# Scoring the short ranges of a gated linear recurrence with 32x32 products in four column groups

## The chip, the cores and the metric

The kernel runs on one NeuronCore of a Trainium2 chip. The metric is the device time of one execution in microseconds (us). Each core has a matrix engine (TensorE, PE in the profile, with its weight loads shown as PEld), a vector engine (DVE), a scalar engine (ACT), a general engine (POOL) and a queue engine (SP). Matrix products write to PSUM, which is eight banks of 512 float32 columns on 128 partitions. Three executions of the kernel before took 1450.94, 1452.36 and 1452.39 us.

## The reference

One residual block of a hybrid encoder: 1024 tokens, 1024 channels, float32. The normalised input is projected to two branches. The first is a stick-breaking attention with 8 heads. The second, around which the change lies, is a gated linear recurrence (HGRN2) with 4 heads of 128 channels:

```python
bcum = jnp.cumsum(gi, axis=2)
diff = bcum[:, :, :, None, :] - bcum[:, :, None, :, :]
decay = jnp.exp(jnp.where(causal[:, :, None], diff, -jnp.inf))
scores = jnp.einsum('bhtd,bhsd,bhtsd->bhts', qi, ki, decay)
o = jnp.einsum('bhts,bhse->bhte', scores, vi) \
    + jnp.einsum('bhtd,bhde->bhte', qi * jnp.exp(bcum), state)
```

Here `gi` is the logarithm of the forget gate, `ki` one minus the gate, and a state is carried from chunk to chunk. Both branches are gated, added and projected, and a squared-ReLU MLP (1024 to 4096 to 1024) and a norm follow.

## The kernel before, in words

Everything is transposed so that channels lie on partitions and tokens in columns; the recurrence works in 8 chunks of 128 tokens. Most products split each float32 operand into a high and a low part of type float32r and add three products (`three`, L526). The recurrence's score products are taken in plain float32.

Within a chunk the score of a pair (s, t) carries the product of the gates between them. The kernel builds it level by level (`hg_levels`, L969). At level l blocks of 2H tokens, H = 2^l, are halved. A key in the left half has been multiplied by the gates up to the end of its half, a query in the right half by the gates from its start, so a plain product of left keys with right queries gives the scores between the halves. After it, `k`, `q` and the running gate products in `dec` are multiplied on DVE for the next level (L1055 to L1057), in two halves of 512 tokens. Seven levels (H = 1 to 64) and the diagonal make a chunk complete. The score tile `sc` has 8 chunks of 128 columns.

The parts of a head before are these. The diagonal and the levels H = 1 and 2 (l = 0 and 1; the sums of a level are formed and laid in the step after it) multiply pairs element by element on DVE (`pairs_of`, L987), split the result in high and low, and sum over channels by a product with a 128x128 tile of ones (`sums_of`, L995). The diagonal's sums are multiplied by the identity into `sc`, and those of l = 0 and 1 are laid by a predicated copy (`lay`, L1010). Levels l = 2, 3, 4 (H = 4, 8, 16) take the whole 128x128 product of each chunk (`scores_of`, L976) and keep the part under a mask (L1070). Levels l = 5 and 6 (H = 32, 64) take only the blocks between halves, as 32x32 and 64x64 products that all write PSUM partitions from 0 upward (L1044), and ACT copies them into `sc` (L1076). `make_masks` (L936) builds the masks once.

Two lanes set PE's order. Blocks opened with `open_block("main")` follow each other as written; blocks of `fill` (the projections, the merge gate's products and others, kept in a stream of jobs) are let in between by a manual dependency on an earlier main block. After each `yield` of the levels or of the tail, the loop at L2168 advances the stream by `FILL[h]` steps (3.75 for the first head); a step of a projection is 2 of 8 channel tiles, 6 passes on PE. The tail of head h - 1 (`hg_tail`, L1079) alternates with the levels of head h: it turns keys, builds the chunk states, multiplies `sc` with the values, normalises (POOL takes the root) and gates. Tiles of 1024 columns come from a pool of 40 slots, tiles of up to 512 columns from a pool of 10; a new tile waits for the release of the one whose place it takes. `turn_lo[0]` is the last remainder that the attention issues on DVE.

Of the kernel before, what the change touches and what calls it, by code (L numbers as in the profile page):

```python
# [9 lines left out]
F32 = mybir.dt.float32  # L10
F32R = mybir.dt.float32r
I32 = mybir.dt.int32
U8 = mybir.dt.uint8
AF = mybir.ActivationFunctionType
ALU = mybir.AluOpType
# [4 lines left out]
P = 128  # L20
T = 1024
D = 1024
NT = T // P
# [16 lines left out]
def kernel(  # L40
# [19 lines left out]
    nc = tc.nc  # L60
# [7 lines left out]
    cpool = ctx.enter_context(tc.tile_pool(name="consts", bufs=1))  # L68
# [6 lines left out]
    def slot(name, dt=F32):  # L75
        return spool.tile([P, 1024], dt, tag="s", name=name)

    def slot_n(name, n, dt=F32):

        if n <= 512:  # L80
            return hpool.tile([P, 512], dt, tag="h", name=name)
        return slot(name, dt)

    def bank(name):
        return psum.tile([P, 512], F32, tag="p", name=name)
# [12 lines left out]
    def after(ins, earlier):  # L98
        if earlier is not None and earlier.ins is not ins.ins:
            tc.add_manual_dep(ins.ins, earlier.ins.name, NOSYNC, reason="issue order")  # L100
        return ins
# [18 lines left out]
    def matmul(*a, **k):  # L120
        return pe(nc.tensor.matmul(*a, **k))  # L121
# [30 lines left out]
    def hi_lo(h, l, src):  # L152
        hi_copy(h, src)
        return lo_sub(l, src, h)

    def mul(out, a, b):
        return nc.vector.tensor_tensor(out=out, in0=a, in1=b, op=ALU.mult)  # L157

    def halves():
        return ((i, slice(i * 512, (i + 1) * 512)) for i in range(2))  # L160

    ident = cpool.tile([P, P], F32, tag="ident", name="ident")
# [764 lines left out]

    hg_jobs(0)

    ones = cpool.tile([P, P], F32R, tag="ones", name="ones")  # L930
    nc.gpsimd.memset(ones.bitcast(F32), 1.0)


    masks = []

    def make_masks():  # L936
        mscr = slot_n("mscr", 4 * P, I32)
        m_x, m_s, m_gt, m_odd = (mscr[:, i * P : (i + 1) * P] for i in range(4))
        nc.gpsimd.iota(m_x, pattern=[[1, P]], base=0, channel_multiplier=0)
        nc.gpsimd.iota(m_s, pattern=[[0, P]], base=0, channel_multiplier=1)  # L940
        nc.vector.tensor_tensor(out=m_gt, in0=m_x, in1=m_s, op=ALU.is_gt)
        nc.vector.tensor_scalar(out=m_odd, in0=m_s, scalar1=1, scalar2=None, op0=ALU.bitwise_and)
        nc.vector.tensor_tensor(out=m_x, in0=m_x, in1=m_s, op=ALU.bitwise_xor)

        def add_mask(l, m_if):
            nc.vector.tensor_scalar(
                out=m_s, in0=m_x, scalar1=l, scalar2=None, op0=ALU.logical_shift_right
            )
            m = bits[:, len(masks) * P : (len(masks) + 1) * P]
            nc.vector.scalar_tensor_tensor(  # L950
                out=m, in0=m_s, scalar=1.0, in1=m_if, op0=ALU.is_equal, op1=ALU.mult
            )
            masks.append(m)

        for l in (0, *range(2, 5)):
            add_mask(l, m_gt)

        mul(m_odd, m_odd, m_gt)
        add_mask(1, m_odd)
        nc.vector.tensor_tensor(out=m_odd, in0=m_gt, in1=m_odd, op=ALU.subtract)  # L960
        add_mask(1, m_odd)

    def chunks(t):
        return t.rearrange("p (c t) -> p c t", t=P)

    def over_chunks(t):
        return t.unsqueeze(1).to_broadcast([P, 4, P])

    def hg_levels(h):  # L969

        dec, k, q = (hg[h, n] for n in ("pp", "k", "q"))
        sc = hg[h, "sc"] = slot(f"sc{h}")

        def scores_of(name):  # L976
            open_block("main")
            banks = []
            for half in range(2):
                S = bank(f"{name}_{half}")  # L980
                for c in range(4):
                    cs = slice((4 * half + c) * P, (4 * half + c + 1) * P)
                    matmul(S[:, c * P : (c + 1) * P], k[:, cs], q[:, cs], start=True, stop=True)
                banks.append(S)
            return banks

        def pairs_of(name, n, *products):  # L987

            t, h_, l_ = (slot_n(f"{name}_{x}", n, d) for x, d in zip("xhl", (F32, F32R, F32R)))
            for (a, b, w), (i, cs) in zip(products, halves()):  # L990
                mul(t[:, cs].rearrange("p (n c) -> p n c", c=w) if w else t[:, 0:n], a, b)
            after(hi_lo(h_, l_, t), turn_lo[0] if "sd0" in name else None)
            return name, n, h_, l_

        def sums_of(pairs):  # L995

            name, n, h_, l_ = pairs
            open_block("main")
            banks = []
            for c0 in range(0, n, 512):  # L1000
                S = bank(f"{name}_{c0}")
                matmul(S, ones, h_[:, c0 : c0 + 512], start=True, stop=False)
                matmul(S, ones, l_[:, c0 : c0 + 512], start=False, stop=True)
                banks.append(S)
            return banks

        def blocks_of(t, H):
            return t.rearrange("p (n two h) -> p n two h", two=2, h=H)

        def lay(mask, S, H):  # L1010

            right = sc.rearrange("p (c n two h) -> p c n two h", c=NT, two=2, h=H)[:, :, :, 1]
            m = blocks_of(mask, H)[:, :, 1].unsqueeze(1).to_broadcast([P, NT, P // (2 * H), H])
            nc.vector.copy_predicated(
                right, m, S.rearrange("p (c n h) -> p c n h", c=NT, h=H)
            )

        pairs = pairs_of(f"sd{h}", T, (k, q, 0))
        for _, cs in halves():
            mul(q[:, cs], q[:, cs], dec[:, cs])  # L1020
        yield
        for l in range(7):
            H = 1 << l
            n = 512 // (2 * H)
            blocks = range(0, P, 2 * H)
            if l <= 2:
                sums = sums_of(pairs)
            if l == 0:
                pairs = pairs_of(
                    f"sl{h}_{l}", 512, (blocks_of(k, 1)[:, :, 0, 0], blocks_of(q, 1)[:, :, 1, 0], 0)  # L1030
                )
            elif l == 1:
                kv, qv = blocks_of(k, 2)[:, :, 0], blocks_of(q, 2)[:, :, 1]
                pairs = pairs_of(
                    f"sl{h}_{l}",
                    T,
                    *((kv[:, :, i : i + 1].to_broadcast([P, T // 4, 2]), qv, 2) for i in (1, 0)),
                )
            elif l < 5:
                banks = scores_of(f"sl{h}_{l}")  # L1040
            else:
                open_block("main")
                S = bank(f"sl{h}_{l}")
                for i, s0 in enumerate(c * P + b for c in range(NT) for b in blocks):  # L1044
                    matmul(
                        S[0:H, i * H : (i + 1) * H],
                        k[:, s0 : s0 + H],
                        q[:, s0 + H : s0 + 2 * H],
                        start=True,
                        stop=True,  # L1050
                    )
            for half_, cs in halves():
                kv, qv, dv = (blocks_of(t[:, cs], H) for t in (k, q, dec))
                left, right = (dv[:, :, i, H - 1 : H] for i in range(2))
                mul(kv[:, :, 0, :], kv[:, :, 0, :], right.to_broadcast([P, n, H]))  # L1055
                mul(qv[:, :, 1, :], qv[:, :, 1, :], left.to_broadcast([P, n, H]))
                hg_level[0] = mul(right, right, left)  # L1057
            if l == 0:
                for i, cs in halves():
                    mul(chunks(sc[:, cs]), chunks(sums[i]), over_chunks(ident))  # L1060
            elif l == 1:
                lay(masks[0], sums[0], 1)
            elif l == 2:
                for m, S in zip(masks[-2:], sums):
                    lay(m, S, 2)
            if l < 2:
                pass
            elif l < 5:
                for half_, cs in halves():
                    nc.vector.copy_predicated(  # L1070
                        chunks(sc[:, cs]), over_chunks(masks[l - 1]), chunks(banks[half_])
                    )
            else:
                for i, b in enumerate(blocks):
                    src = S[0:H].rearrange("p (c b t) -> p c b t", c=NT, t=H)[:, :, i, :]
                    nc.scalar.copy(chunks(sc)[b : b + H, :, b + H : b + 2 * H], src)  # L1076
            yield

    def hg_tail(h):  # L1079
# [1207 lines left out]
```

## Time and profile before

| | |
|---|---|
| runs | 1450.94, 1452.36, 1452.39 us |
| the profiled execution, its span | 1450.94 us, equal to the lowest run |
| PE busy | 1436.3 us |
| DVE busy | 1100.4 us |
| ACT busy | 668.9 us |
| POOL busy | 143.9 us |
| the recurrence | from about 316 to 588 us |

A row of a group names the source line, the engine, the operation, the tile written and the tiles read, the tile shape of the array (rows*columns), the operands' form and the count; then the busy time of the group in us, the mean of one in ns, and the engine's idle time just before them. Nearly all matmuls carry line L121, that of a helper, so they are told apart by their tiles: `sd` is the diagonal, `sl` a level. A row of the timeline starts with the start and the duration in us. Matmuls overlap one another, so the distance of starts is their price and not their duration.

### The profile page before, as it was taken

What the parts mean: (1) busy time and instruction counts of PE and PEld (TensorE: products, weight loads), DVE (VectorE), ACT (ScalarE), POOL (GpSimd) and SP (SyncE); (2) the same over time, 40 slices, a digit from 0 to 9 for tenths busy, and PEclk for the clock granted to TensorE, in tenths of its full rate; (3) what the DMA queues carried; (4) which work ended last, traced back from release to release, by engine and by line L of the source; (5) the groups of instructions that cost most, each with busy time, mean ns of one, the idle gap of its engine ahead of it and who ended that gap; (6) DMA issues with size and microseconds to landing.
All of it is one profiled execution on the core that took longest, in us unless ns stands there. A gap on an engine that the chain in (4) does not pass through costs nothing.

```text
span 1450.9 us, 19987 instructions
## 1 busy us (share of the span) xinstructions
PE 1436.3 (99%) x7470; PEld 1223.2 (84%) x7470; DVE 1100.4 (76%) x1571; ACT 668.9 (46%) x1156; POOL 143.9 (10%) x340
## 2 busy tenths in 40 slices
PE   9999999999999999999999999999999999999998
PEld 8989988988898888888877888888888888888886
DVE  6699899798746797887757898666666757768765
ACT  7566666652323243523344575444444533523443
POOL 3121121110000012100010200000000000000032
PEclk9999999999999999999999999999999999999999
DMA  7234154321303349655478414444445975676735
GB/s 211 49 97 104 37 95 81 59 44 51 102 16 102 73 142 263 226 168 177 142 219 302 162 65 147 144 159 152 152 160 185 346 272 183 250 268 251 276 102 187
DMA packets 157913, 225.73 MB, mean 156 GB/s; under 512 B 25676, under 2 KB 93816, under 8 KB 157816
## 3 DMA queue, kind: packets, MB, share of 16 engines
q1 hardware_dynamic: 142552, 183.29, 37.8%
q0 software_dynamic: 11520, 34.61, 9.6%
q10 hardware_dynamic: 3744, 6.56, 1.2%
q8 instruction: 59, 0.97, 0.3%
q14 instruction: 38, 0.31, 0.1%
HBM read 162.55 MB, written 61.87 MB: 155 GB/s over the span
## 4 chain that ended last, share of the span: by engine, by line
PE 90%; DVE 4%; issue 3%; DMA 2%; ACT 1%; POOL 1%; SPq 0%; POOLq 0%; DVEq 0%; ACTq 0%
PE pm L121 21%; PE pX L121 9%; PE pW L121 6%; PE pY L121 6%; PE pjqk L121 6%; PE pji L121 3%; PE pys L121 3%; PE pga L121 3%; PE pjg L121 2%; PE po L121 2%; PE pjv L121 2%; PE z L121 2%; PE pjf L121 2%; PE pjq L121 2%; PE gX L121 2%
## 5 line engine op out<-in xcount | busy, mean ns | idle before, releaser
L144 ACT CAST whid<-w 128x1024 fp32r<-128x1024 f32 x30 | 31.6, 1053 | 153.7 <-PE pm L121 89.5
L777 DVE TENSOR_TENSOR_SCAN rm<-rm,bits 128x511 f32<-128x511 f32 (+7 forms) x72 | 87.3, 1219 | 14.2 <-ACT rm L755 12.8
L121 PE MATMUL pm<-wlod,sh 128*128 128x512 f32 x240 | 93.5, 390 | 0.0
L121 PE MATMUL pm<-whid,sh 128*128 128x512 f32 x240 | 93.4, 389 | 0.0
L121 PE MATMUL pm<-whid,sl 128*128 128x512 f32 x240 | 93.4, 389 | 0.0
L121 PE MATMUL pm<-tl,sh 128*128 128x512 f32 (+1 forms) x210 | 81.3, 387 | 0.0
L121 PE MATMUL pm<-th,sl 128*128 128x512 f32 (+1 forms) x210 | 81.3, 387 | 0.0
L121 PE MATMUL pm<-th,sh 128*128 128x512 f32 (+1 forms) x210 | 81.3, 387 | 0.0
L149 DVE TENSOR_TENSOR wlod<-w,whid 128x1024 fp32r<-128x1024 f32 x30 | 36.6, 1221 | 53.3 <-ACT whid L144 53.2
L149 DVE TENSOR_TENSOR sl<-sa,sh 128x1024 fp32r<-128x1024 f32 x56 | 68.2, 1217 | 0.5 <-ACT sh L144 0.5
L144 ACT CAST wTh<-pw 128x128 fp32r<-128x128 f32 (+3 forms) x96 | 44.4, 487 | 50.3 <-PE pw L124 42.7
L1936 POOL TENSOR_SCALAR fss<-fss 128x1 f32<-128x1 f32 x8 | 4.5, 562 | 562.1 <-ACT fsc L1931 561.6
L144 ACT CAST sh<-sa 128x1024 fp32r<-128x1024 f32 x56 | 57.2, 1046 | 6.2 <-DMA sa<-ad 6.2
L149 DVE TENSOR_TENSOR wTl<-pw,wTh 128x512 fp32r<-128x512 f32 (+3 forms) x96 | 50.7, 547 | 8.8 <-ACT wTh L144 6.3
L121 PEld LDWEIGHTS pm<-wlod,sh 128*128 128x128 f32 x240 | 45.0, 187 | 9.9 <-DVE wlod L149 0.4
L121 PEld LDWEIGHTS pm<-whid,sh 128*128 128x128 f32 x240 | 45.1, 188 | 9.3
L121 PEld LDWEIGHTS pm<-whid,sl 128*128 128x128 f32 x240 | 45.0, 188 | 9.3
L157 DVE TENSOR_TENSOR bt<-bt,rm 128x511 f32<-128x511 f32 (+7 forms) x72 | 48.9, 685 | 5.0 <-ACT bt L758 1.0
L121 PE MATMUL pX<-sql,t1h 128*128 128x512 f32 x128 | 50.0, 391 | 0.1
L121 PE MATMUL pX<-sqh,t1l 128*128 128x512 f32 x128 | 49.8, 389 | 0.0
L121 PE MATMUL pX<-sqh,t1h 128*128 128x512 f32 x128 | 49.8, 389 | 0.0
L755 ACT ACTIVATE rm<-z 128x511 f32<-128x511 f32 (+6 forms) x96 | 47.6, 503 | 4.5 <-DVE bt L157 1.9
(923 smaller groups left out, 4598.5 us busy)
## 6 DMA issues: line engine op xcount, KB each, us to landing
w<-in_w_ff_dram SPq DMA_DIRECT2D x72, 512.0 KB, 5.4
sa<-ad SPq DMA_DIRECT2D x56, 512.0 KB, 6.6
ad<-a SPq DMA_DIRECT2D x32, 256.0 KB, 4.2
ad<-s SPq DMA_DIRECT2D x16, 512.0 KB, 5.7
tw<-in_w_out_dram POOLq DMA_DIRECT2D x24, 256.0 KB, 4.1
x<-in_x_dram SPq DMA_DIRECT2D x8, 512.0 KB, 8.6
xnl<-xnh POOLq DMA_DIRECT2D x8, 512.0 KB, 11.7
pr<-pd SPq DMA_DIRECT2D x8, 512.0 KB, 6.1
```

The lines of the kernel that those rows point to most:

```text
L121: return pe(nc.tensor.matmul(*a, **k))
L144: hi_last[0] = after(in_turn("act", nc.scalar.copy(dst, src)), hi_behind[0])
L149: nc.vector.tensor_tensor(out=dst, in0=src, in1=hi.bitcast(F32), op=ALU.subtract),
L157: return nc.vector.tensor_tensor(out=out, in0=a, in1=b, op=ALU.mult)
L755: nc.scalar.activation(rm[:, s0 + c0 - 1 : s0 + m - 1], z[:, c0:m], AF.Sigmoid, scale=-0.125)
L777: sc = nc.vector.tensor_tensor_scan(out=rr, data0=rr, data1=bits[:, 1024 - nk + a : 1024 - nk + b][:, ::-1], initial=rm[:, b : b + 1] if i ...
L1936: nc.gpsimd.tensor_scalar(out=ssq, in0=ssq, scalar1=1.0 / D, scalar2=EPS, op0=ALU.mult, op1=ALU.add)
```

## The change

The tile of ones and the whole route over pair products and sums are gone. The diagonal and levels l = 0 to 4 (H = 1 to 16) now all do the same: for each chunk and each of its four 32-token blocks, one float32 product of that block's keys with that block's queries, 32 in a level. A block that starts at token b of its chunk writes PSUM partitions b to b + 31, so neighbouring products write different 32-column groups of the array, and the results of a chunk lie in 32 columns. A level thus takes one bank with 256 columns. A predicated copy (`keep`) puts what the mask of the level allows into a compact tile `near` of 256 columns, which POOL sets to zero first, as it does `sc`.

For l = 5 the 16 products of 32x32 write at partition 0 or 64, for l = 6 the 8 products of 64x64 at partition 0 or 64 in turn. In the step of l = 5 ACT copies `near` into the four diagonal blocks of `sc` (four copies of 32 partitions) and the level's result (two copies); l = 6 takes two copies of 64 partitions. The decay multiplications take all 1024 tokens at once instead of two halves. The diagonal's products are now issued ahead of the multiplication of `q` with the gates, and its `keep` behind the attention's last remainder. The masks are 32 columns wide, one for each of six steps.

```diff
-    ones = cpool.tile([P, P], F32R, tag="ones", name="ones")
-    nc.gpsimd.memset(ones.bitcast(F32), 1.0)
...
+        near = slot_n(f"near{h}", NT * Q)[:, 0 : NT * Q]
+        nc.gpsimd.memset(near, 0.0)
+        nc.gpsimd.memset(sc, 0.0)
+
+        def scores_of(l, size, firsts, where):
             open_block("main")
...
+            S = bank(f"sl{h}_{l}")
+            for i, (s0, t0) in enumerate(firsts):
+                r0, c0 = where(i, s0)
+                matmul(
+                    S[r0 : r0 + size, c0 : c0 + size],
+                    k[:, s0 : s0 + size],
+                    q[:, t0 : t0 + size],
+                    start=True,
+                    stop=True,
+                )
+            return S
+
+        def near_scores(l):
+            at = [c * P + b for c in range(NT) for b in range(0, P, Q)]
+            S = scores_of(l, Q, [(s0, s0) for s0 in at], lambda i, s0: (s0 % P, s0 // P * Q))
+            return chunks(S[:, 0 : NT * Q], Q)
+
+        def keep(l, S):
+            return nc.vector.copy_predicated(chunks(near, Q), masks[l], S)
...
-        pairs = pairs_of(f"sd{h}", T, (k, q, 0))
-        for _, cs in halves():
-            mul(q[:, cs], q[:, cs], dec[:, cs])
+        S = near_scores("d")
+        mul(q, q, dec)
+        after(keep(5, S), turn_lo[0])
         yield
         for l in range(7):
...
+            if l < 5:
+                S = near_scores(l)
+            elif l == 5:
+                S = scores_of(
+                    l,
+                    H,
+                    [(s0, s0 + H) for s0 in range(0, T, 2 * H)],
+                    lambda i, s0: (s0 % P, s0 // P * H),
+                )
+            else:
+                S = scores_of(
+                    l,
+                    H,
+                    [(s0, s0 + H) for s0 in range(0, T, 2 * H)],
+                    lambda i, s0: (i % 2 * H, i // 2 * H),
+                )
+            kv, qv, dv = (blocks_of(t, H) for t in (k, q, dec))
+            left, right = (dv[:, :, i, H - 1 : H] for i in range(2))
+            mul(kv[:, :, 0, :], kv[:, :, 0, :], right.to_broadcast([P, n, H]))
+            mul(qv[:, :, 1, :], qv[:, :, 1, :], left.to_broadcast([P, n, H]))
+            hg_level[0] = mul(right, right, left)
+            if l < 5:
+                keep(l, S)
+            elif l == 5:
+                for b in range(0, P, Q):
+                    nc.scalar.copy(chunks(sc)[b : b + Q, :, b : b + Q], chunks(near, Q)[b : b + Q])
+                for b in range(0, P, 2 * H):
+                    nc.scalar.copy(
+                        chunks(sc)[b : b + H, :, b + H : b + 2 * H],
+                        chunks(S[b : b + H, 0 : NT * H], H),
+                    )
+            else:
+                for i in range(2):
+                    nc.scalar.copy(
+                        sc.rearrange("p (c two t) -> p c two t", two=2, t=P)[0:H, :, i, H:P],
+                        chunks(S[i * H : (i + 1) * H, 0 : 4 * H], H),
+                    )
```

More of the change, by code (lines that the diff above doesn't have):

```diff
@@ L928 @@
     hg_jobs(0)
-    ones = cpool.tile([P, P], F32R, tag="ones", name="ones")
-    nc.gpsimd.memset(ones.bitcast(F32), 1.0)
     masks = []
+    Q = 32
     def make_masks():
[L937 to L940, printed above, removed]
+        mscr = slot_n("mscr", 4 * Q, I32)
+        m_x, m_s, m_gt, m_t = (mscr[:, i * Q : (i + 1) * Q] for i in range(4))
+        nc.gpsimd.iota(m_x, pattern=[[1, Q]], base=0, channel_multiplier=0)
+        nc.gpsimd.iota(m_s, pattern=[[0, Q]], base=0, channel_multiplier=1)
+        nc.vector.tensor_scalar(
+            out=m_s, in0=m_s, scalar1=Q - 1, scalar2=None, op0=ALU.bitwise_and
+        )
@@ L941, in make_masks @@
         nc.vector.tensor_tensor(out=m_gt, in0=m_x, in1=m_s, op=ALU.is_gt)
-        nc.vector.tensor_scalar(out=m_odd, in0=m_s, scalar1=1, scalar2=None, op0=ALU.bitwise_and)
         nc.vector.tensor_tensor(out=m_x, in0=m_x, in1=m_s, op=ALU.bitwise_xor)
[L945 to L967, printed above, removed]
+        for l in range(6):
+            m = bits[:, l * Q : (l + 1) * Q]
+            if l < 5:
+                nc.vector.tensor_scalar(
+                    out=m_t, in0=m_x, scalar1=l, scalar2=None, op0=ALU.logical_shift_right
+                )
+                nc.vector.scalar_tensor_tensor(
+                    out=m, in0=m_t, scalar=1.0, in1=m_gt, op0=ALU.is_equal, op1=ALU.mult
+                )
+            else:
+                nc.vector.tensor_scalar(
+                    out=m, in0=m_x, scalar1=0, scalar2=None, op0=ALU.is_equal
+                )
+            masks.append(m.unsqueeze(1).to_broadcast([P, NT, Q]))
@@ L969, in hg_levels, with chunks @@
+    def chunks(t, n=P):
+        return t.rearrange("p (c t) -> p c t", t=n)
     def hg_levels(h):
@@ L974, in hg_levels @@
         sc = hg[h, "sc"] = slot(f"sc{h}")
-        def scores_of(name):
+        near = slot_n(f"near{h}", NT * Q)[:, 0 : NT * Q]
+        nc.gpsimd.memset(near, 0.0)
+        nc.gpsimd.memset(sc, 0.0)
+        def scores_of(l, size, firsts, where):
             open_block("main")
[L978 to L1005, printed above, removed]
+            S = bank(f"sl{h}_{l}")
@@ L1007, in blocks_of @@
+        def keep(l, S):
+            return nc.vector.copy_predicated(chunks(near, Q), masks[l], S)
         def blocks_of(t, H):
             return t.rearrange("p (n two h) -> p n two h", two=2, h=H)
[L1010 to L1016, printed above, removed]
@@ L1023, in hg_levels @@
             H = 1 << l
[L1024 to L1030, printed above, removed]
-                )
[L1032 to L1037, printed above, removed]
-                )
[L1039 to L1071, printed above, removed]
-                    )
-            else:
-                for i, b in enumerate(blocks):
-                    src = S[0:H].rearrange("p (c b t) -> p c b t", c=NT, t=H)[:, :, i, :]
-                    nc.scalar.copy(chunks(sc)[b : b + H, :, b + H : b + 2 * H], src)
+            n = 512 // H
@@ new lines, in hg_levels @@
+            kv, qv, dv = (blocks_of(t, H) for t in (k, q, dec))
[3 more added lines that the diff above has]
+            hg_level[0] = mul(right, right, left)
+            if l < 5:
+                keep(l, S)
[6 more added lines that the diff above has]
+                        chunks(S[b : b + H, 0 : NT * H], H),
+                    )
+            else:
+                for i in range(2):
+                    nc.scalar.copy(
+                        sc.rearrange("p (c two t) -> p c two t", two=2, t=P)[0:H, :, i, H:P],
+                        chunks(S[i * H : (i + 1) * H, 0 : 4 * H], H),
+                    )
```

## The prediction

> **What bounds the kernel now.** I read the busy shares and the chain of waits first, then who makes TensorE (PE) wait, then the stage of the change, then single blocks of it. From the page:
>
> ```profile
> PE 1436.3 (99%) x7470; PEld 1223.2 (84%) x7470; DVE 1100.4 (76%) x1571; ACT 668.9 (46%) x1156; POOL 143.9 (10%) x340
> ...
> PE 90%; DVE 4%; issue 3%; DMA 2%; ACT 1%; POOL 1%; SPq 0%; POOLq 0%; DVEq 0%; ACTq 0%
> ```
>
> A busy PE need not be a PE at its limit, so the waits of PE in the whole execution, and two slices of the recurrence (busy us of PE, PEld, DVE, ACT, POOL, then the granted clock):
>
> ```profile
> PE pwW L121 <- DVE h L1186: 4.5, 1, 4.5
> PE warm L121 <- POOL ident masks.py:199: 2.2, 1, 2.2
> PE sl L121 <- DVE q L157: 0.2, 1, 0.2
> ```
>
> ```profile
> 320.00:340.00 20.00, 20.00 (x104) 17.06 (x103) 19.97 (x44) 3.56 (x5) 0.00 (x0) 1.00 0.10 28
> 340.00:360.00 20.00, 19.82 (x136) 16.22 (x135) 16.13 (x39) 6.36 (x11) 0.00 (x0) 1.00 0.19 53
> ```
>
> In the whole recurrence PE waited for DVE once, 0.2 us. DVE is as full as PE between 320 and 340 us, yet PE didn't wait there: the projections that fill between the blocks cover it. So this stage costs what its matmuls take to pass, and I count passes. By form, from 300 to 590 us, all four heads together (count, busy us, mean ns):
>
> ```profile
> L121 PE MATMUL sl<-q,k 128*128 128x128 f32 x192 | 23.5, 275 | 0.2 <-DVE q L157 0.2
> ...
> L121 PE MATMUL sl<-q,k 128*32 128x32 f32 x128 | 4.8, 197 | 0.0
> ...
> L121 PE MATMUL sl<-sl_h,ones 128*128 128x512 f32 x12 | 4.7, 390 | 0.0
> L121 PE MATMUL sl<-sl_l,ones 128*128 128x512 f32 x12 | 4.7, 389 | 0.0
> L121 PE MATMUL sl<-q,k 128*64 128x64 f32 x64 | 4.6, 225 | 0.0
> ...
> L121 PE MATMUL sd<-sd_h,ones 128*128 128x512 f32 x8 | 3.1, 389 | 0.0
> ```
>
> The mean durations overlap, so they are no prices. The counts are: 192 passes are 4 heads x 3 levels x 8 products x 2, and 128 are 4 x 16 x 2. **One float32 product is two passes**, a product with the ones (fp32r) is one; `sd_l` has the count of `sd_h`.
>
> **Prices on PE, from starts.** Passes of 512 columns (four sums of the diagonal among them), then a block of each float32 form between two such passes (start us, us):
>
> ```profile
> 319.49 0.39 PE L121 MATMUL pjf<-xnh,wf1l 128*128 128x512 f32 x1
> ...
> 320.62 0.39 PE L121 MATMUL pjf<-xnh,wf1h 128*128 128x512 f32 x1
> ```
>
> ```profile
> 338.51 0.39 PE L121 MATMUL pjq<-xnh,wq1l 128*128 128x512 f32 x1
> 338.74 1.95 PE L121 MATMUL sl<-q,k 128*128 128x128 f32 x16
> 340.44 0.48 PE L121 MATMUL pjg<-xnh,wg1h 128*128 128x512 f32 x1
> 340.76 0.40 PE L121 MATMUL pjg<-xnl,wg1h 128*128 128x512 f32 x1
> ```
>
> ```profile
> 350.74 0.39 PE L121 MATMUL pjg<-xnh,wg1l 128*128 128x512 f32 x1
> 351.06 1.20 PE L121 MATMUL sl<-q,k 128*32 128x32 f32 x32
> 352.19 0.50 PE L121 MATMUL pjg<-xnh,wg1h 128*128 128x512 f32 x1
> 352.52 0.39 PE L121 MATMUL pjg<-xnl,wg1h 128*128 128x512 f32 x1
> ```
>
> ```profile
> 356.17 0.39 PE L121 MATMUL pga<-xnh,wga0wlo 128*128 128x512 f32 x1
> 356.49 1.15 PE L121 MATMUL sl<-q,k 128*64 128x64 f32 x16
> ...
> 357.90 0.39 PE L121 MATMUL pga<-xnl,wga0whi 128*128 128x512 f32 x1
> ```
>
> (320.62 - 319.49)/5 = 0.227 us for a pass of 512. A block's cost is the time from the last pass ahead of it to the second behind it, less 2 x 0.227 = 0.454: the 128-wide block costs 340.76 - 338.51 - 0.454 = 1.80 us, the 32-wide one 1.33, the 64-wide one 1.28. The pace inside a block is its busy time less one mean duration, over the steps: (1.95 - 0.275)/15 = 112 ns, (1.15 - 0.225)/15 = 61.7, (1.20 - 0.197)/31 = 32.4. So 16 x 112 ns = 1.80 explains the wide block whole, but 32 x 32.4 ns = 1.04 leaves 0.29 us of the small one, and 16 x 61.7 = 0.99 leaves 0.29 as well: **a block in a narrower tile shape pays 0.29 us** for going in and out.
>
> The pace falls by (112 - 32.4)/96 = 0.83 ns a column, with 6 ns that don't. Weight loads, on their own row:
>
> ```profile
> 352.19 0.19 PEld L121 LDWEIGHTS pjg<-xnh,wg1h 128*128 128x128 f32 x1
> 352.29 0.19 PEld L121 LDWEIGHTS pjg<-xnl,wg1h 128*128 128x128 f32 x1
> ```
>
> Right behind the small block two loads of 128 columns start 0.10 us apart, about 0.8 ns a column: 26.4 ns for 32 columns at 0.83. I read the small block as paced by its loads, 26.4 ns each and 6 ns of changing over; moving columns fall in the same ratio, so this is a reading and not proved.
>
> **Removed from PE, per head:** 4 diagonal sums (0.91 us), 2 and 4 sums of levels 1 and 2 (0.45 + 0.91), three wide blocks (3 x 1.80 = 5.40): 7.67 us.
>
> **Added, per head:** six blocks (diagonal, levels 1 to 16), each 8 chunks x 4 products x 2 = 64 passes of 32 columns, four times the passes of a wide block. Neighbouring products now lie in different column groups; nothing in this trace does that. Without any effect of it the pace stays 32.4 ns; if the next group's load need not wait for the last multiply, it falls to the bare load, 26.4. I take the middle, 29.4: 64 x 0.0294 + 0.29 = 2.17 us a block, 13.03 for six. Levels 32 and 64 keep their 32 and 16 passes; 3 ns each off is 0.15 us. Sum: 13.03 - 7.67 - 0.15 = +5.2 us a head, **+20.8 us for four**. The ends: 32.4 gives 4 x (6 x 2.36 - 7.67) = +26.1, 26.4 gives 4 x (6 x 1.98 - 7.67 - 0.29) = +15.7.
>
> A rule speaks for a floor close by. The Trainium skill, "TensorEngine Tiling (Array Packing)", Instruction Overhead, says that a matmul has about 60 cycles of overhead, so that one moving column lasts as long as 60, and warns against taking a tiling factor from a dimension that is small already; 32 moving columns are. At the 2.4 GHz of "TensorE: Matmul & The Clock Gate" that is an estimate of 25 ns a pass, and the sum would be about +13 us. The trace's 32.4 ns lies above it and doesn't contradict it.
>
> **The other engines.** Rows of the same window:
>
> ```profile
> L157 DVE TENSOR_TENSOR k<-k,pp 128x256 f32<-128x256 f32 x56 | 23.5, 420 | 8.4 <-PE sl L121 8.4
> L1070 DVE COPY_PREDICATED sc<-bits,sl 128x512 f32<-128x512 uint8 x24 | 16.6, 730 | 0.0
> L1014 DVE COPY_PREDICATED sc<-bits,sl 128x512 f32<-128x512 uint8 x12 | 15.7, 1312 | 0.1
> L157 DVE TENSOR_TENSOR q<-q,pp 128x512 f32<-128x512 f32 x8 | 5.3, 682 | 0.0
> ```
>
> ```profile
> L1076 ACT COPY sc<-sl 32x256 f32<-32x256 f32 x8 | 2.9, 361 | 6.2 <-PE sl L121 6.1
> ```
>
> ```profile
> L811 POOL MEMSET wTh<- 128x128 f32 x2 | 0.4, 202 | 0.5 <-PE po L121 0.5
> ```
>
> DVE loses the predicated copies (16.6 + 15.7 us), all pair products and remainders, and half its decay multiplies in number: 2 x 420 ns become one of 682, 28 times for k and 28 for q, about 9 us. It gains 24 keeps of 256 columns, under 730 ns each. That is over 24 us off DVE even at the 730, and worth between nothing and the 0.2 us that PE waited: I take nothing. ACT exchanges three casts a head for eight copies of 64 or 32 partitions, about 361 ns each, far below its room. POOL gets two memsets a head, about 8 x 202 ns and 2 x 202 ns. If the big one has to wait for its slot, POOL's statistics of the tail and its DMA issues stand behind it, and after them DVE's normalising; PE's fill covers that up to several us, so 0, with 2 us as the upper end.
>
> New waits: DVE's decay of q now follows the diagonal's block on PE, and each keep stands in front of the next level's multiplies. DVE already waits for the blocks (8.4 us in the k row) at no cost to PE. A level's chain is now about 2.2 us of PE, two multiplies of 0.68 and a keep, near 4.3 us; 3.75 fill steps of 6 passes x 0.227 = 5.1 us stand between two levels of head 0. That cover is thinner than before, hence 1 us more at the upper end.
>
> **Sum.** The profiled execution's span is 1450.94 us, which is also the lowest of the three runs; their median is 1.4 us above. 1450.94 + 20.8 = 1471.8, as a median 1473.
>
> **Rivals.**
> *The groups run beside each other.* For it: nothing in the rows forbids it, since every small block now writes the first group alone. Against: one PEld row whose loads follow each other at 0.8 ns a column. With four groups at once the pace is 32.4/4 = 8.1 ns: six blocks cost 6 x (0.52 + 0.29) = 4.85; levels 32 and 64 use two groups and lose half their passes' time, 0.52 + 0.49; 4.85 - 7.67 - 1.01 = -3.83 a head, -15.3 in all: 1437 as a median. At half the pace (16.2 ns) it is 4 x (7.96 - 7.67 - 1.01) = -2.9, 1449.5. It decides from about 18 ns a pass downward. The Trainium skill's page on tiling, Key Properties, says exactly this, that different tiles can load and multiply in parallel; no run here shows it yet.
>
> *Loads and multiplies follow each other* instead of overlapping, when group changes with every product: 26.4 + 26.4 + 6 = 59 ns, 4 x (6 x 4.05 - 7.67) = +66 us, 1519. Against it: loads overlap multiplies inside the present block.
>
> *DVE was the hidden limit* and its relief pays. The 19.97 us of 20 speak for it, the single wait of 0.2 us against it; at most 0.4 us, inside the bound of no change only if the passes came out even.
>
> **How the numbers follow.** Load pace: 58 in 100, 1468 to 1478.5, likeliest 1473. Groups in parallel: 30, 1437 to 1447. Half pace: 5, near 1449.5. Loads and multiplies in turn: 5. The rest, 2, slower by something else. Load pace alone is not 8 in 10, so the range takes in the parallel case: 1437 to 1480 with the 1 us and part of the 2 us above. Faster by over 0.2% (2.9 us, about what a measurement tells from no change) 0.30, within 0.05, slower 0.65.
>
> **What would show it.** Right: the rows of the 32-wide form go from 128 to 1664 passes; blocks of 64 take near 64 x 29 ns from first to last start with 0.3 us around them; PE still waits for nothing; DVE's busy time falls by tens of us while the span grows. Wrong: blocks of 64 under 1.1 us (groups in parallel), or near 3.8 us (in turn), or PE waiting for the keep, for `near` or for a memset.

## The result: 1 per cent faster, by the rival that was given 30 in 100

The changed kernel takes 1438.01 us (median; 1437.39 to 1439.29), the kernel before 1452.38 (1450.94 to 1453.47). The ratio is 0.9903, 95% interval 0.9889 to 0.9917, that is 12 to 16 us less. The forecast was 1473. The rival in which the column groups run beside each other was put at 1437.

From the page of the changed kernel: busy us and shares; then who makes PE wait in the whole execution.

```profile
PE 1421.1 (99%) x8774; PEld 1202.9 (84%) x8774; DVE 1048.5 (73%) x1432; ACT 666.7 (46%) x1164; POOL 148.4 (10%) x347
```

```profile
PE pwW L121 <- DVE h L1150: 4.4, 1, 4.4
PE warm L121 <- POOL ident masks.py:199: 2.2, 1, 2.2
PE pjqk L121 <- DVE xnl L325: 0.3, 1, 0.3
PE sl L121 <- DVE q L157: 0.2, 1, 0.2
```

PE has 1304 passes more than before and is busy 15.2 us less. It still waits for nothing in the recurrence but DVE's q, once, 0.2 us. DVE lost 51.9 us. The groups by form (the recurrence's stage), then one near block, one of level 32 and one of level 64 between passes of 512 columns (start us, us):

```profile
L121 PE MATMUL sl<-q,k 128*32 128x32 f32 x1408 | 18.0, 199 | 0.2 <-DVE q L157 0.2
...
L121 PE MATMUL sl_d<-q,k 128*32 128x32 f32 x256 | 3.0, 199 | 0.0
L121 PE MATMUL sl<-q,k 128*64 128x64 f32 x64 | 2.7, 228 | 0.0
```

```profile
319.56 0.39 PE L121 MATMUL pjf<-xnh,wf1l 128*128 128x512 f32 x1
319.88 0.76 PE L121 MATMUL sl<-q,k 128*32 128x32 f32 x64
320.57 0.51 PE L121 MATMUL pjf<-xnh,wf1h 128*128 128x512 f32 x1
320.91 0.39 PE L121 MATMUL pjf<-xnl,wf1h 128*128 128x512 f32 x1
```

```profile
347.42 0.39 PE L121 MATMUL pjg<-xnh,wg1l 128*128 128x512 f32 x1
347.74 0.70 PE L121 MATMUL sl<-q,k 128*32 128x32 f32 x32
...
348.70 0.39 PE L121 MATMUL pjg<-xnl,wg1h 128*128 128x512 f32 x1
```

```profile
352.36 0.39 PE L121 MATMUL pga<-xnh,wga0wlo 128*128 128x512 f32 x1
352.68 0.69 PE L121 MATMUL sl<-q,k 128*64 128x64 f32 x16
...
353.62 0.39 PE L121 MATMUL pga<-xnl,wga0whi 128*128 128x512 f32 x1
```

Read as the prediction reads such blocks, with its passes of 0.227 us taken off: the near block costs 320.91 - 319.56 - 0.454 = 0.90 us, and its pace is (0.76 - 0.199)/63 = **8.9 ns a pass** (one group before: 32.4). Level 32, with two groups in turn, costs 0.83 us (1.33 before) at (0.70 - 0.199)/31 = 16.2 ns. Level 64, in two groups, costs 0.81 us (1.28) at (0.69 - 0.228)/15 = 30.8 ns (61.7). Four groups divide the pace by 3.6, two by two. Summed with the 7.67 us a head that the prediction took off: 4 x (6 x 0.90 - 7.67 - 0.50 - 0.47) = -13.0 us, inside the measured interval.

Once more, beside the last three experiments, the changed kernel took 1438.27 us and a ratio of 0.9913 (0.9899 to 0.9928):

> The changed kernel once more, on the same chip as the three runs beside it: 1438, ratio near 0.990.

### The profile page after: what moved, and what is told of

Its sections match the earlier page's. It is cut to its first block, busy times and chain, and to the rows that moved or that the text cites. A ratio compares the mean times of both kernels' runs of the same rounds, so it can differ in the third digit from the quotient of the medians.

```text
span 1435.7 us, 22472 instructions
## 1 busy us (share of the span) xinstructions
PE 1421.1 (99%) x8774; PEld 1202.9 (84%) x8774; DVE 1048.5 (73%) x1432; ACT 666.7 (46%) x1164; POOL 148.4 (10%) x347
## 4 chain that ended last, share of the span: by engine, by line
PE 95%; DMA 1%; issue 1%; POOL 1%; DVE 1%; ACT 1%; SPq 0%; POOLq 0%; DVEq 0%
PE pm L121 21%; PE pX L121 9%; PE pW L121 6%; PE pY L121 6%; PE pjqk L121 6%; PE pji L121 3%; PE pga L121 3%; PE pjq L121 3%; PE pjf L121 3%; PE pys L121 3%; PE gX L121 3%; PE pyh L121 3%; PE gY L121 3%; PE pjg L121 3%; PE po L121 3%; PE z L121 2%
```

## The experiments

Two theories stood against each other. **G**: neighbours in different column groups load and multiply beside each other. **F**: the small blocks are fast through their form (64 products of tokens that lie together), whatever the groups.

The kernel before, timed again beside the experiments, took 1451.58, 1450.95 and 1451.34 us (medians of 7, 1 and 13 executions) against 1452.38 above, so times from different sets of runs compare to about 1.5 us.

### One group after the other

```diff
-            at = [c * P + b for c in range(NT) for b in range(0, P, Q)]
+            at = [c * P + b for b in range(0, P, Q) for c in range(NT)]
```

> The changed kernel with one thing different: the 32 products of a near block (diagonal, levels 1 to 16) are issued group by group, eight to one column group before the next, instead of group after group. Same products, same PSUM places. Theory G (neighbours in different column groups load and multiply beside each other, so the pace is the one-group pace of 32.4 ns over the number of groups among neighbours): the pace of a block returns to about 32 ns, a block costs 64 x 0.032 + 0.33 = 2.4 us against 0.90 now, 24 blocks x 1.48 = +35 us, about 1473. Rival F (the pace comes from the block's form, many products of the same 32 tokens, and not from the groups): 8.9 ns as now, 1438.

Measured: 1467.21 us, ratio to the kernel before 1.0106 (1.0090 to 1.0121). The same products to the same places, 29.2 us slower than the changed kernel, and slower than the kernel before. A block of it:

```profile
321.40 0.39 PE L121 MATMUL pjf<-xnh,wf1l 128*128 128x512 f32 x1
321.72 1.91 PE L121 MATMUL sl<-q,k 128*32 128x32 f32 x64
...
323.89 0.39 PE L121 MATMUL pjf<-xnl,wf1h 128*128 128x512 f32 x1
```

It costs 2.04 us, 1.14 more, and 24 x 1.14 = 27 us. The products are the same and the gain is gone, so the form alone doesn't make it. But neighbours in the sorted order also come from different chunks, and this run by itself doesn't part the groups from tokens that lie together; the run with levels 32 and 64 in one group does. The 2.4 us of the expectation were a little high: the pace over the whole block is (1.91 - 0.199)/63 = 27 ns and not 32, because around each change of group some passes start about 5 ns apart, the new group's among the old one's.

### Two groups in turn

```diff
-            at = [c * P + b for c in range(NT) for b in range(0, P, Q)]
+            at = [c * P + b0 + b for b0 in (0, 2 * Q) for c in range(NT) for b in (0, Q)]
```

> The changed kernel with the near products alternating between two column groups (0 and 1 for all chunks, then 2 and 3). Theory G: pace 32.4/2 = 16 ns, a block 64 x 0.0162 + 0.33 = 1.37 us, 24 x 0.47 = +11 us, about 1449. Rival F: 1438.

Measured: 1446.63 us (one run), 8.6 above the changed kernel.

```profile
332.06 0.39 PE L121 MATMUL pjq<-xnh,wq1l 128*128 128x512 f32 x1
332.38 1.11 PE L121 MATMUL sl<-q,k 128*32 128x32 f32 x64
...
333.75 0.39 PE L121 MATMUL pjq<-xnl,wq1h 128*128 128x512 f32 x1
```

The block costs 1.24 us, 0.34 more than with four groups (24 x 0.34 = 8.2 us), at (1.11 - 0.199)/63 = 14.5 ns. One, two and four groups among neighbours give 27, 14.5 and 8.9 ns, as G has it.

### Levels 32 and 64 in one group

The products of both levels write from partition 0 on, and ACT copies them as before the change.

```diff
-                    lambda i, s0: (s0 % P, s0 // P * H),
...
-                    lambda i, s0: (i % 2 * H, i // 2 * H),
+                    lambda i, s0: (0, i * H),
...
```

> The changed kernel with levels 32 and 64 written to PSUM partitions from 0 on, as the kernel before has them, and ACT's copies of them as there. Theory G: their blocks go back from 0.83 and 0.81 us to 1.33 and 1.28, 4 x 0.97 = +3.9 us, about 1442. Rival: these blocks are hidden or their saving is eaten by the copies, 1438.

Measured: 1442.48 us, ratio 0.9937 (0.9921 to 0.9954), 4.5 us above the changed kernel. Level 32:

```profile
347.49 0.39 PE L121 MATMUL pjg<-xnh,wg1l 128*128 128x512 f32 x1
347.81 1.20 PE L121 MATMUL sl<-q,k 128*32 128x32 f32 x32
...
349.28 0.39 PE L121 MATMUL pjg<-xnl,wg1h 128*128 128x512 f32 x1
```

The sorted run kept the places and changed the order; here the products and their order are those of the changed kernel, and on PE only the place in PSUM differs. The block is back at 349.28 - 347.49 - 0.454 = 1.34 us and (1.20 - 0.199)/31 = 32.3 ns, where two groups in turn gave 0.83 us and 16.2 ns; level 64 is back at 1.28 us and 61.5 ns. Neither the form nor the order of tokens can explain this, so F falls, and the groups of the neighbours are the cause. Spreading these two levels is about a third of the gain; the rest comes from the near blocks and what they replace.

### What the multiply costs beside the load

The prediction read the small block as paced by its weight loads. Here each product streams its 32 query columns twice; the loads stay as they are. First with the groups sorted, then with four in turn.

```diff
...
+                    qs = qs.unsqueeze(1).to_broadcast([P, times, size])
+                    dst = dst.rearrange("p (n t) -> p n t", t=size)
...
```

> As the run with products sorted by group, and each product streams its 32 query columns twice, into 64 columns of PSUM, of which the first 32 are used. Loads are unchanged, only the multiply doubles. Theory W (in one group the weight load sets the pace): the pace stays near 32 ns and the time that of the sorted run, about 1473. Rival M (the multiply takes 0.83 ns a column as well, so it is the bound as soon as it is wider): 64 x 0.83 + 6 = 59 ns, a block 4.1 us, 24 x 3.2 = +77 us against the changed kernel, about 1515.

> The changed kernel, four groups in turn, with the doubled multiply of the run before. Theory W: loads set the pace, 8.9 ns as now, 1438. Rival M: 59/4 = 15 ns, a block 64 x 0.0148 + 0.33 = 1.28 us, 24 x 0.38 = +9 us, about 1447. If the multiplies of different groups did not overlap at all, 53 ns a pass, 24 x 2.8 = +68 us, about 1506.

Measured: 1497.18 us sorted, 1446.10 us with four groups (one run each).

```profile
329.76 0.39 PE L121 MATMUL pjf<-xnh,wf1l 128*128 128x512 f32 x1
330.08 3.18 PE L121 MATMUL sl<-q,k 128*32 128x64 f32 x64
...
333.52 0.40 PE L121 MATMUL pjq<-xnl,wq1h 128*128 128x512 f32 x1
```

```profile
332.03 0.39 PE L121 MATMUL pjq<-xnh,wq1l 128*128 128x512 f32 x1
332.35 1.10 PE L121 MATMUL sl<-q,k 128*32 128x64 f32 x64
...
333.71 0.40 PE L121 MATMUL pjq<-xnl,wq1h 128*128 128x512 f32 x1
```

Theory W falls in both. Sorted, a block costs 3.31 us and the mean pace is (3.18 - 0.2)/63 = 47 ns with the overlaps at the changes of group; if the loads set the pace, it would have stayed at 2.04 us. Away from the changes of group the trace has a pass every 56 ns, and every 32 ns in the sorted run with single columns. So in a float32 pass the multiply has a price by its columns as well. The first two loads of a sorted block start 28 ns apart, so at 32 by 32 load and multiply are about equal, and the rows before could not tell them apart. With four groups the doubled multiply costs 1.23 us a block at (1.10 - 0.2)/63 = 14.3 ns, so multiplies do run beside each other across groups. In the changed kernel both loads and multiplies must overlap across groups, since 8.9 ns lies far below 28 and 32.

### The change of tile shape

One 128x128 product more in each near block, in its middle, and as a control behind it.

```diff
+                if len(firsts) == 32 and i == 16:
+                    matmul(S[:, 256:384], ident, ident, start=True, stop=True)
```

> The changed kernel with one product of 128x128 more (the identity with itself, two float32 passes of 112 ns, into unused columns of the bank) in the middle of each near block. Theory S (going to another tile shape and back costs 0.33 us): 24 x (0.224 + 0.33) = +13 us, about 1451. Rival (the 0.33 us belongs to the start and end of a float32 block, whatever its shapes): 24 x 0.224 = +5 us, about 1443.

> The control of the run before: the same 128x128 product behind each near block instead of in its middle, so that the shape changes as often as in the changed kernel. Theory S: 24 x 0.224 = +5 us, about 1443. The difference to the run before is the price of 24 changes of shape there and back, 8 us by theory S and 0 by the rival.

Measured: 1450.27 us in the middle, 1445.37 us behind (one run each).

```profile
326.33 0.39 PE L121 MATMUL pjf<-xnh,wf1l 128*128 128x512 f32 x1
326.65 0.46 PE L121 MATMUL sl<-q,k 128*32 128x32 f32 x32
327.04 0.49 PE L121 MATMUL sl<-ident 128*128 128x128 f32 x2
327.46 0.46 PE L121 MATMUL sl<-q,k 128*32 128x32 f32 x32
327.85 0.50 PE L121 MATMUL pjq<-xnh,wq1h 128*128 128x512 f32 x1
328.18 0.39 PE L121 MATMUL pjq<-xnl,wq1h 128*128 128x512 f32 x1
```

```profile
325.02 0.39 PE L121 MATMUL pjf<-xnh,wf1l 128*128 128x512 f32 x1
325.33 0.76 PE L121 MATMUL sl<-q,k 128*32 128x32 f32 x64
326.03 0.49 PE L121 MATMUL sl<-ident 128*128 128x128 f32 x2
...
326.59 0.40 PE L121 MATMUL pjq<-xnl,wq1h 128*128 128x512 f32 x1
```

The blocks cost 328.18 - 326.33 - 0.454 = 1.40 and 326.59 - 325.02 - 0.454 = 1.12 us. The same product is 0.28 us dearer where it changes the shape once more there and back. Theory S holds; 24 x 0.28 = 6.7 us against 4.9 between two single runs (four runs of the changed kernel lie 2 us apart).

### DVE's relief

Eleven multiplications of 128x1024 a head into a tile that nobody reads, placed behind the diagonal's keep and behind each level's decay multiplications and keep: all heads, then heads 0 to 2, then head 3 alone.

```diff
+            for _ in range(2 if l < 3 else 1):
+                mul(idle, dec, dec)
```

> The changed kernel with DVE's relief taken back: 11 multiplications of 128x1024 a head (about 1.22 us each, 54 us in all; DVE's busy time fell by 52) into a tile that nobody reads, spread over the steps of the levels. Theory G with PE as the only bound: no change, 1438 within 1 us. Rival R (part of the gain is DVE's relief): slower by what PE's passes don't account for, 1 to 2 us, or by more if it was the main cause.

> The DVE load of the earlier run (11 multiplications of 128x1024 a head), but in heads 0 to 2 only, 40 us. If that run lost its 8 us in one place, the tail of the last head, where a late weight load stood ahead of DVE's copy for the keys: no change, 1438. If DVE's relief is worth something everywhere: 6 of the 8 us, 1444.

> The same load in head 3 only, 13 us. If the loss lies in that one place: about 1446, with one wait of PE for ACT's copy of the turned keys of about 6 us. If the load acts everywhere: a quarter of the 8 us, 1440.

Measured: 1446.19 us with all heads loaded (ratio 0.9961, 0.9947 to 0.9976), 1438.61 with heads 0 to 2 (0.9917, 0.9902 to 0.9932), 1448.15 with head 3 (0.9972, 0.9959 to 0.9985; 1440.66 to 1450.05). The first run went against the forecast of no change, and the other two place it: 40 us of DVE work in the first three heads cost nothing, 13 us in the last cost 8 to 10 (in one of ten runs only 2.4). From the run with all heads loaded: PE's wait, the slice 540 to 560 us of it and then of the changed kernel, and the timeline of ACT, DVE and PE ahead of the wait.

```profile
PE pkv L121 <- ACT pp L1061: 6.3, 1, 6.3
```

```profile
540.00:560.00 20.00, 13.94 (x103) 10.14 (x101) 13.39 (x19) 8.72 (x15) 4.78 (x6) 0.97 1.06 256
560.00:580.00 20.00, 18.92 (x98) 16.67 (x99) 13.07 (x21) 8.94 (x25) 5.06 (x6) 0.86 0.59 193
```

```profile
540.00:560.00 20.00, 20.00 (x145) 16.54 (x144) 13.48 (x24) 7.91 (x15) 6.08 (x8) 1.00 1.07 260
```

```profile
555.70 1.04 ACT L144 CAST wo01h<-wo01r 128x1024 fp32r<-128x1024 f32 x1 [8.93 <-DMA wo01r<-in_w_o_sb_dram]
...
556.78 1.23 DVE L149 TENSOR_TENSOR wo01l<-wo01r,wo01h 128x1024 fp32r<-128x1024 f32 x1 [6.42 <-ACT wo01h L144]
...
560.19 0.17 DVE L1052 COPY fc<-pp 128x8 f32<-128x8 f32 x1
...
560.45 0.97 ACT L1061 COPY pp<-pk 128x512 f32<-128x512 f32 x2 [2.21 <-DVE fc L1052]
```

It is one chain. A weight tile lands late, ACT's split of it waits 8.93 us and DVE's remainder 6.42, DVE's small copy `fc` for the tail stands behind that in order, ACT's copy of the turned keys waits for `fc`, and PE for this copy. The issue of that load stands at 540.1 us in this run and lands 15.5 us later; in the changed kernel it is issued at 536.0 and lands in 7.1, in slices in which the DMA engines are full in both kernels. PE's wait is followed by a slice at a granted clock of 0.86. The load goes into the buffer that `wga7r` held, and DVE's last read of that, `wga7t`, ends at 540.1 us in this run and at 535.6 in the changed kernel: the added work on DVE sends the load out later. Why it then takes twice as long to land isn't shown. In the kernel before, with about the same total of DVE work, PE has no such wait that the relief could have taken away, so the relief is not part of the gain; it is a margin at one place.

### Both prices put to use

```diff
+        raw = q
...
-        S = near_scores("d")
-        mul(q, q, dec)
-        after(keep(5, S), turn_lo[0])
+        q = hg[h, "q"] = slot(f"qd{h}")
+        after(mul(q, raw, dec), turn_lo[0])
         yield
+        keep(5, near_scores("d"))
...
-                    lambda i, s0: (s0 % P, s0 // P * H),
+                    lambda i, s0: (i % 4 * H, i // 4 * H),
```

> The changed kernel with the two things that the runs so far price. Level 32 goes round four column groups instead of two (16 ns a pass become 8.5: 4 x 32 x 0.0077 = -1.0 us). The decay of q writes a tile of its own, so that the diagonal (old q) and level 1 (new q) follow each other without projections between and share one change of tile shape (4 x 0.3 = -1.2 us). If theory G and the price of the shape change hold: 2.2 us under the changed kernel, about 1436. Rival: the gain is under the noise or is lost to two more ACT copies a head, 1438.

Measured: 1435.59 us (1435.09 to 1436.36), ratio 0.9895 (0.9880 to 0.9910), 2.7 us under the changed kernel in the same comparison, whose runs lie between 1437.14 and 1439.54. The two intervals of the ratio overlap, the runs themselves don't. The forecast was 2.2 less, and the trace has both parts of it. The diagonal and level 1 of the first head:

```profile
318.56 0.39 PE L121 MATMUL pjf<-xnh,wf1l 128*128 128x512 f32 x1
318.88 0.76 PE L121 MATMUL sl_d<-q,k 128*32 128x32 f32 x64
319.49 0.75 PE L121 MATMUL sl<-qd,k 128*32 128x32 f32 x64
...
320.51 0.40 PE L121 MATMUL pjf<-xnl,wf1h 128*128 128x512 f32 x1
```

The two blocks cost 320.51 - 318.56 - 0.454 = 1.50 us together, where two apart cost 1.80, and level 32 costs 0.59 us in place of 0.83: 4 x (0.30 + 0.24) = 2.2 us.

It is the fastest version that was run.

## Why the prediction was wrong

**What bounds the stage: right.** In the runs that change only PE's products the time moved with their passes; only the load on DVE moved it by a wait, at one place. Adding up blocks from starts gave 27, 8.2 and -13.0 us where the clock gave 29.2, 8.6 and -14.4.

**Removed from PE: kept.** The 7.67 us a head enter the sum above unchanged; no run measures them by themselves, and the sum misses 1.4 of the 14.4 us.

**Added, per head: the step that failed.** It took the pace of a small block to lie between 32.4 ns ("without any effect" of the groups) and 26.4 ns ("the bare load"), and so treated the loads of four groups as one queue. Measured are 8.9 ns. A near block costs 0.90 us and not 2.17, six blocks 5.4 and not 13.0 us: 7.6 us a head, 30 of the 35 us between forecast and result. The lower bound came from a row in which two loads of 128 columns follow each other; both load the whole array, so the row says nothing of two loads into different groups. No row of the trace before did, and then the bound had to be left open downward. The rule of the Trainium skill that the prediction set beside the sum, from "TensorEngine Tiling (Array Packing)", Instruction Overhead, pulled the same way: the estimate of 25 ns a pass that was made from it doesn't hold as a floor across groups, where the runs show 8.9. What the Trainium skill says in the same page's Key Properties, that different tiles load and multiply in parallel, is what the runs show.

**Levels 32 and 64: the same error.** They were given 0.15 us a head; two groups halve their pace and bring 0.50 + 0.47, and the run without their spreading confirms 4.5 us in all. That is another 3.3 us.

**The price of the tile shape: right.** 0.29 us was read from two blocks of the kernel before; the changed kernel shows 0.90 - 64 x 0.0089 = 0.33, and the pair of runs made for it 0.28.

**The reading that loads set the pace: undecided then, half right.** Load and multiply cost about the same at 32 by 32 (28 and 32 ns).

**The other engines at nothing: right for this change, with a thinner cover than was said at one place.** No new wait of PE arose in the recurrence. But work on DVE isn't free everywhere, as the load in the last head shows.

**The base.** An execution takes about 1.8 us more than its span (1437.51 and 1435.7 for the profiled run), so the span before was not that of the lowest run, as the prediction took it; this moves the forecast by under 1 us.

The likeliest case was chosen wrongly. The rival's own working (a quarter of the pace, two groups for the far levels, 1437) has the mechanism and came within about 1 us, in part by luck: its pace of 8.1 ns was a little too fast, six blocks at 4.85 and not 5.4 us a head, 2.2 us in all, which about makes up for the 1.4 us that the blocks don't explain.

## What to carry to other kernels

Where many small products follow each other on PE, look at which column groups neighbours write: issue them in turn over the groups, and the pace divides by nearly the number of groups (2 by two, 3.6 by four here); the same products sorted by group lost 29 us here. Price a block from the starts around it, the cost of changing the tile shape apart, and let blocks of the same shape follow each other. A bound for an operation that the trace doesn't have holds only if the row it comes from uses the same part of the hardware.

## What the hardware showed unexpectedly

Starts of passes in different groups can lie 5 to 7 ns apart, and groups run ahead of one another: even sorted by group, passes around a change of group interleave. A float32 pass in one group costs about 32 ns at 32 by 32, and doubling the moving columns alone raised a sorted block from 2.04 to 3.31 us. Going into a narrower tile shape and back cost 0.28 to 0.33 us in the blocks priced here, whatever was done inside. And one wait of 6.3 us on PE was followed by a slice of 20 us at a mean granted clock of 0.86, and the loss (8 us) was more than the wait.
